# First feed-forward layer in emission order on TensorE, VectorE and ScalarE

## The chip, the cores and the metric

The kernel runs as one program on one NeuronCore of one Trainium2 chip. The metric is the device time of that program in microseconds, start to end on the chip. A short word on the engines, as the profile names them: PE is TensorE (the matrix engine; PEld is its weight load), DVE is VectorE, ACT is ScalarE, POOL is GpSimd, SP is SyncE, which here issues the DMA loads. Each engine works through its own instruction stream in the order in which the stream was written, and waits on semaphores where an instruction needs something from another engine or from a DMA.

## The reference

A two-layer encoder on 256 tokens of 2048 features, all in float32. The layer that the change touches is the channel mixer of layer 0:

```python
def conv_ffn(h, w_up, conv_w, conv_b, w_down):
    gate, up = jnp.split(h @ w_up, 2, axis=-1)
    gp = jnp.pad(gate, ((0, 0), (1, 1), (0, 0)))
    gate = gp[:, :-2] * conv_w[0] + gp[:, 1:-1] * conv_w[1] + gp[:, 2:] * conv_w[2] + conv_b
    return (jax.nn.gelu(gate, approximate=True) * up) @ w_down

for layer in range(DEPTH):                                  # DEPTH = 2
    mod = cond @ ada_w[layer] + ada_b[layer]                # 2048 x 12288, one row
    sh1, sc1, g1, sh2, sc2, g2 = split(mod, 6)
    h = rms_norm(x, norm_g[layer, 0]) * (1.0 + sc1) + sh1
    y = local_dilated_mixer(...) if layer == 0 else diff_attention(...)
    x = x + g1 * rms_norm(y, norm_g[layer, 1])
    h = rms_norm(x, norm_g[layer, 2]) * (1.0 + sc2) + sh2
    y = conv_ffn(h, ...)                                    # hidden width 5504
    x = x + g2 * rms_norm(y, norm_g[layer, 3])
```

## The kernel before

**Weights.** Every weight is read once from HBM. The matrices are cut into *units* of 128 x 1024 float32 (512 KB). A unit is loaded by SP into one of nine `raw` buffers (`load`, L232), split by ACT into a high part `whi` (L259, a rounding copy) and by DVE into the rest `wlo` = `raw` - `whi` (L309), and then used by PE in three matmuls for each product: high times high, high times low, low times high. There are four `whi` and four `wlo` buffers (`SPLIT_BUFS`), so a unit's split can only begin when PE has finished the unit four places earlier; a `raw` buffer is free when its `wlo` is made.

**Modulation.** The rows `mod` are one-row products. They are made from *modulation units*, 128 x 1024 of `ada_w`, also 512 KB and also loaded into the nine `raw` buffers (L236); DVE multiplies each by a column of the condition and adds it to `aacc` (L284; the first of sixteen is L296, or L305 after a start on POOL in L299). Two ticks after the sixteenth, PE sums the partitions (L459 for columns, L451 for gate rows) and DVE takes the result (L471, L474, L453).

**Order.** `Plan.order` writes one list `seq` in which weight units ("w") and modulation units ("a") alternate; in the layer of the change there are 128 "a" to 215 "w", and the last 20 units of the layer have none among them. Loads go out in this order, at most nine ahead (`prefetch`). The program is written as a stream of units: after PE's matmuls of a unit comes `done`, which frees the split buffer, calls `advance` (use up the next entries of `seq`: the copy to `whi` for one "w", the addition to `aacc` for each "a" up to the next "w"), then `tick` (run what is due of the work put off by `chain` and `at`), then `lows` (the `wlo` whose `whi` was just written):

```python
        def done(self, i):
            self.free(i)
            self.advance(lows=False)
            self.tick()
            self.lows()
```

`ada` itself also calls `lows` right after its addition, so where a "w" is followed by an "a", the order written is `whi`, `aacc`, `wlo`, and then the work of the tick.

**The layer.** `ffn(0, ...)` works in two parts of 22 and 21 feature tiles. For each pair of tiles it makes a gate product and an up product (four units each, `feat_units`, matmuls L655, L657, L658 with 256 columns), and then the down product of the part (`out_chunks` with `tok_units`, L622 to L624 with 512 columns, four chunks of 512). The gate product is read from PSUM by ACT (L1051), gets its two outer taps from DVE (L1040, L1042, one tick later), and its gelu from ACT (L1046, two ticks later). The up product is multiplied with it on DVE (L1058), copied to the high part by ACT (L1059) and split by DVE (L1060), a tick apart. The first 7 products (`PRE = 7`) of the layer are made in another loop, in three steps over the contraction; from the eighth on a product is made over its full contraction (L1082 to L1097). Each chunk of the down product is taken by ACT (L1105) in the first part, and by DVE with a sum of squares on ACT (L1108, L491) in the second. The last chunk of the second part ends in `tail`, which makes the norms and the first products of the next layer.

**What sets the order on the engines.** The program is traced into a list of instructions; a list scheduler then decides each engine's order. It runs its own model of the time that each instruction takes, and gives an engine, whenever it is free, the earliest-written instruction that is ready in the model. Within `tc.manual_schedule(engines=ORDERED)`, PE, DVE and ACT instead get the order in which the instructions were written; SP and POOL stay with the list scheduler. In this kernel that is done in one place only, around `tail` (L911).

Of the kernel before, what the change touches and what calls it, by code (L numbers as in the profile page):

```python
# [3 lines left out]

# [5 lines left out]
F32 = mybir.dt.float32  # L10
F32R = mybir.dt.float32r
I32 = mybir.dt.int32
AF = mybir.ActivationFunctionType
# [3 lines left out]
D, S, P = 2048, 256, 128  # L17
KT = D // P
# [19 lines left out]


class Plan:  # L40
    """The order in which weight units and modulation units reach the chip."""

    def __init__(self, ab_w_in, ab_w_out, c_w_in, c_w_out, ffn_w_up, ffn_w_down):
        self.units = []
# [41 lines left out]
                               .rearrange("(a p) n -> p a n", p=P), b, n))  # L86

    def token_chunks(self, w, ks, late=0, lc=2, last=False):
        """512 columns at a time; of the first lc chunks, the last units come after all others"""
        pairs = [ks[i:i + 2] for i in range(0, len(ks), 2)]  # L90
        head = pairs[:len(pairs) - late]
        order = [(ch, head) for ch in range(lc)] + [(ch, pairs[len(head):]) for ch in range(lc)]
        order += [(ch, pairs) for ch in range(lc, 4)]
        for ch, ps in order:
            n = len(self.units)
            for p in ps:
                self.rows(w, p[0], len(p), ch * 512, 512)
            if last and ch == 3:
                u = len(self.units) - n
                skew = min(u, SPLIT_BUFS + HELD)  # L100
                self.held |= set(range(n + u - skew, n + u - SPLIT_BUFS))
# [47 lines left out]
        assert self.ia == len(self.ada)  # L149

    def put(self, nw, na, p=1.0):
        """nw weight units with na modulation units spread among them"""
        e = self.ia + na
        for k in range(nw):
            t = e - na + round(na * ((k + 1) / nw) ** p)
            while self.ia < t:
                self.seq.append(("a", self.ia))
                self.ia += 1
            self.seq.append(("w", self.iw))
            self.iw += 1  # L160
        while self.ia < e:
            self.seq.append(("a", self.ia))
            self.ia += 1
# [25 lines left out]
def encoder_kernel(ctx: ExitStack, tc: tile.TileContext, x, c, ada_w, ada_b, norm_g,  # L189
                   ab_w_in, ab_w_out, a_sink, c_w_in, c_w_out, c_lambda, c_subln_g,  # L190
                   ffn_w_up, ffn_conv_w, ffn_conv_b, ffn_w_down, out):
    nc = tc.nc
# [12 lines left out]
    def vy():  # L205
        return cp.tile([P, 2, D], F32, name="vy")
# [4 lines left out]
    class Stream:  # L211
# [98 lines left out]
            self.los = []  # L310

        def advance(self, limit=None, lows=True, n=None):
            """use up what has been loaded, as far as the split buffers reach"""
            if n is not None:
                limit = self.used + n
            while self.used < len(seq) and (limit is None or self.used < limit):
                kind, i = seq[self.used]
                if kind == "w":
                    if i in plan.held:
                        if self.held_tile is None:  # L320
                            break
                    elif i in plan.native:
                        if self.direct == DIRECT:
                            break
                    elif self.outstanding == SPLIT_BUFS:
                        break
                if kind == "a" and i in plan.gated:
                    if not self.gate:
                        break
                    self.gate -= 1  # L330
                s = self.used
                self.used += 1
                if kind == "w":
                    self.split(s, i)
                else:
                    self.ada(s, i)
                self.prefetch()
            if lows:
                self.lows()
# [9 lines left out]
            return i, self.hl.pop(i)  # L349

        def open(self, n):
            """let n of the gated modulation units through"""
            self.gate += n
            self.advance()

# [15 lines left out]
            self.later.append((self.now + ticks, age, fn))  # L371

        def chain(self, *stages, delay=0):
            """stages one tick after another, each given what the one before returned; older chains go first"""
            age = self.age = self.age + 1

            def run(k, v):
                r = stages[k](v)
                if k + 1 < len(stages):
                    self.at(1, lambda: run(k + 1, r), age)  # L380
            self.at(1 + delay, lambda: run(0, None), age)
# [12 lines left out]
    st = Stream()  # L394
    mods, cur = {}, {}

# [1 line left out]
    def rows_tile():  # L398
        return tmp.tile([P, P], F32, name="crow", bufs=2)

# [33 lines left out]
    nc.vector.memset(mhalf, -0.5)  # L434
    nc.scalar.activation(crow[:KT, :], crow[:KT, :], AF.Silu)

# [1 line left out]
    def gate_rows(l, m):  # L438
        mods[l, m] = cp.tile([P, D], F32, name="gb")
        i0 = 1 if m == 2 else 3  # L440
# [32 lines left out]
                g0 = (l * 4 + (0 if m == 1 else 2)) * KT + k0  # L473
                nc.vector.scalar_tensor_tensor(col, col, 1.0, ngc[:, g0:g0 + n], op0=ALU.add, op1=ALU.mult)  # L474

# [1 line left out]
    def sums():  # L477
        s = small("ssq", 5)
        nc.gpsimd.memset(s[:, 4:5], EPS)
# [16 lines left out]
        return d  # L496

    class Affine:
        """the modulated rows of feature tiles k.. from src, split into high and low parts"""

        def __init__(self, t, k, src, A, B, act, keep=False):
            n = src.shape[1]
# [29 lines left out]
        return dst  # L532

    def chunk_T(t, ch, r, dst):
        """rows 4 ch.. of the normalised and transposed x"""
        z = normed(t, ch, r, tmp.tile([P, 512], F32, name="hf", bufs=3), True)
        nc.scalar.activation(dst, transposed(z, bank()), AF.Copy)

# [1 line left out]
        cur["hT"] = cp.tile([P, KT, 2, S], F32R, name="hT")  # L540

    class Norm:
        """x += gate * rms_norm(y), then the modulated rms_norm of x, transposed and split, for one token block"""

        def __init__(self, t, y, ssq, A=None, B=None):
            self.t, self.y, self.ssq, self.A, self.B = t, y, ssq, A, B
# [65 lines left out]
                for a in self.half:  # L612
                    a.low()

# [1 line left out]
    def mm_tok(dst, act, kt, t, hi, lo, first, last):  # L616
        if lo is None:
            nc.tensor.matmul(dst, cur["h"][:, kt, t * P:(t + 1) * P], hi, start=first, stop=last,
# [5 lines left out]
        nc.tensor.matmul(dst, al, hi, start=False, stop=last, skip_group_check=True)  # L624

    def tok_units(dsts, act, ks, first=True, last=True, one_bank=False):
        """dsts[t] += act block t times the next weights, rows ks"""
        n = 0
        while n < len(ks):
            i, (hi, lo) = st.take()  # L630
            a = hi.shape[1]
            for b in range(a):
                for t in range(2):
                    mm_tok(dsts[t], act, ks[n + b], t, hi[:, b], lo and lo[:, b],
                           first and n + b == 0 and not (one_bank and t), last and n + b == len(ks) - 1)
            n += a
            st.done(i)

    def feat_units(acc, k0, kn, n):
        """one bank: acc[:, j] += (next weights).T @ h for n // 128 feature tiles"""  # L640
        hT = cur["hT"]
        kt = k0
        while kt < k0 + kn:
# [19 lines left out]
    def packed():  # L663
        return bank().rearrange("p (j n) -> p j n", j=2)

# [1 line left out]
    def feat_out(pool, acc, scale, name, bufs=1):  # L667
        q = pool.tile([P, 2, S], F32, name=name, bufs=bufs)
        nc.scalar.activation(q, acc, AF.Copy, scale=scale)
# [13 lines left out]
                                                        op0=ALU.mult, op1=ALU.subtract)  # L683

    def probs_T(pool, parts):
        """the transposed probabilities: parts[t] lists what is summed, each with its normalising diagonal"""
        pt = bank().rearrange("p (k q) -> p k q", k=2)
        for t in range(2):
            for kt in range(2):
# [170 lines left out]

        st.chain(scores, soft, expo, norm, turn, apply, rstd, scaled, back, finish)

# [1 line left out]
    def out_chunks(act, ks, evac, late=0, lc=2, norms=None, late_mods=False, head=None):  # L864
        pairs = [ks[i:i + 2] for i in range(0, len(ks), 2)]
        n = len(ks) - sum(len(p) for p in pairs[len(pairs) - late:]) if late else len(ks)
# [164 lines left out]
    def ffn(l, pool, next_norm, pre=0, head=None, first=()):  # L1031
# [30 lines left out]
        for part, (f0, fn) in enumerate(PARTS):  # L1062
# [3 lines left out]
            for n, (k0, k1) in enumerate(zip(FK, FK[1:])) if p else ():  # L1066
# [7 lines left out]
                for a in range(p):  # L1074
                    feat_units(accs[a], k0, k1 - k0, 2 * P)
                    if k1 == KT:
# [2 lines left out]
                            gate(accs[a], cv, a, 2)  # L1079
                        else:  # L1080
                            up(accs[a], cv, act, a - 1, 2)
            for j in range(p // 2 * 2, fn, 2):  # L1082
                nj = min(2, fn - j)
                for k in range(2):
                    if j + k < p:
                        continue
                    if first:
                        acc = first.pop()
                        feat_units(acc, 4, KT - 4, nj * P)
                    else:  # L1090
                        acc = packed()
                        feat_units(acc, 0, KT, nj * P)
                    if k == 0:
                        cv = pool.tile([P, 2, S], F32, name="cv", bufs=2)
                        gate(acc, cv, f0 + j, nj)
                    else:
                        up(acc, cv, act, j, nj)  # L1097
            final = part == len(PARTS) - 1
            y = y or vy()

            def evac(acc, t, ch, then=None):
                c0 = ch * 512
                yc = y[:, t, c0:c0 + 512]
                if part == 0:
                    nc.scalar.activation(yc, acc, AF.Copy)  # L1105
                    return
                z = tmp.tile([P, 512], F32, name="hf", bufs=3) if final else yc
                nc.vector.tensor_add(z, acc, yc)  # L1108
                if final:
                    square_sum(z, ssq[t][:, ch:ch + 1])  # L1110
                    nc.vector.tensor_mul(yc, z, mods[l, 5][:, c0:c0 + 512])
                if then:
                    then()

            out_chunks(act, list(range(fn)), evac, 0, 0,
                       (lambda: [next_norm(t, y, ssq[t]) for t in range(2)]) if final else None, head=head)

# [1 line left out]
    v_acc, v_got = [], []  # L1119

    def v_units(t, i, k0, hi, lo):
# [197 lines left out]
```

## Time and profile before

| | |
|---|---|
| median of 3 runs | 2326.51 us (2325.22 to 2333.98) |
| profiled execution: span, first to last instruction | 2334.3 us |
| profiled execution: time around the span | not shown on the page |
| PE busy | 2226.5 us (95%) |
| DVE busy | 1620.0 us (69%) |
| ACT busy | 1055.0 us (45%) |
| DMA moved | 587.14 MB, mean 252 GB/s |
| mean granted TensorE clock | 0.980 |

The profile is of one execution. Busy shares are over the whole span, which has stages with different limits. "Idle before" of a group is how long its engine stood still just before instructions of the group, with what ended the wait. In a table of stretches each row gives the stretch's length, each engine's busy time with its number of instructions, the granted TensorE clock (1.00 is full speed), the share of the time that the 16 DMA engines were busy, and the rate. The busy time of PE counts matmuls that overlap, so PE can look busy while it runs below its pace; the number of matmuls in a stretch tells more.

The layer's part that is changed runs from about 460 us to 1160 us of the span: the 7 early products end at about 460 us, the last chunk of the second part and `tail` lie around 1075 to 1160 us.

### The profile page before, as it was taken

To read this page: it belongs to the slowest core of one execution; us is meant where nothing else is said; L and a number is where in the kernel's file an instruction comes from. 1 tells how busy PE (TensorE), PEld (TensorE's weight loads), DVE (VectorE), ACT (ScalarE), POOL (GpSimd) and SP (SyncE) were. 2 spreads that over 40 slices of the span, in tenths; PEclk is the share of its full clock that TensorE was granted. 3 is DMA by queue.
4 is the path that set the end of the run, shared out by engine and by line. 5 is a ranking of instruction groups with operands and counts; after the bars stand their busy time and mean duration, and the time that the engine had idled before them with its cause. 6 is when DMAs were issued, how large, how long until landed. Compare 5 with 4: busy or idle time off the path is not lost.

```text
span 2334.3 us, 37324 instructions
## 1 busy us (share of the span) xinstructions
PE 2226.5 (95%) x14961; PEld 2030.9 (87%) x14961; DVE 1620.0 (69%) x1802; ACT 1055.0 (45%) x1451; POOL 45.5 (2%) x72
## 2 busy tenths in 40 slices
PE   5689999999999999999999999999999999999998
PEld 3679978999877999987888999888999988999986
DVE  7888987887666677776687886657565545565555
ACT  4334455544333334434554554446444444444443
POOL 0000000000000000000000110000000000000000
PEclk8889999999999999999999999999999999999999
DMA  9999989898778888887589996665677666666652
GB/s 343 367 329 318 327 292 316 294 306 287 249 263 273 277 268 270 273 261 265 177 287 334 308 307 212 212 198 162 200 205 203 199 206 207 193 205 201 178 187 104
DMA packets 390427, 587.14 MB, mean 252 GB/s; under 512 B 18110, under 2 KB 256360, under 8 KB 389612
## 3 DMA queue, kind: packets, MB, share of 16 engines
q1 hardware_dynamic: 390252, 584.75, 77.3%
q8 instruction: 117, 1.92, 0.3%
q14 instruction: 58, 0.48, 0.1%
HBM read 582.58 MB, written 2.10 MB: 250 GB/s over the span
## 4 chain that ended last, share of the span: by engine, by line
PE 58%; DMA 17%; issue 13%; DVE 10%; ACT 1%; POOL 1%; DVEq 0%; POOLq 0%; ACTq 0%
DMA raw<-in_ada_w_dram 14%; PE bank L657 11%; PE bank L655 11%; PE bank L658 11%; PE bank L623 7%; PE bank L622 7%; PE bank L624 7%; DVE wlo L309 4%; DVE aacc L284 4%; DMA raw<-in_ffn_w_down_dram 2%; DMA raw<-in_ffn_w_up_dram 1%; PE bank L459 1%; DMA raw<-in_ab_w_in_dram 1%; PE bank L794 1%; PE bank L523 1%
## 5 line engine op out<-in xcount | busy, mean ns | idle before, releaser
L259 ACT ACTIVATE whi<-raw 128x1024 fp32r<-128x1024 f32 x708 | 740.5, 1053 | 873.9 <-PE bank L657 399.6
L309 DVE TENSOR_TENSOR wlo<-raw,whi 128x1024 fp32r<-128x1024 f32 x708 | 856.9, 1217 | 369.3 <-ACT whi L259 356.6
L658 PE MATMUL bank<-hT,wlo 128*128 128x256 f32 x3616 | 1022.7, 283 | 20.1 <-DVE wlo L309 20.0
L655 PE MATMUL bank<-hT,whi 128*128 128x256 f32 x3616 | 1027.9, 284 | 0.0
L657 PE MATMUL bank<-hT,whi 128*128 128x256 f32 x3616 | 1018.8, 282 | 0.2 <-DVE hT L518 0.2
L658 PEld LDWEIGHTS bank<-hT,wlo 128*128 128x128 f32 x3616 | 685.9, 190 | 26.8 <-DVE wlo L309 26.1
L655 PEld LDWEIGHTS bank<-hT,whi 128*128 128x128 f32 x3616 | 686.4, 190 | 3.1 <-ACT whi L259 1.0
L657 PEld LDWEIGHTS bank<-hT,whi 128*128 128x128 f32 x3616 | 686.1, 190 | 3.2 <-issue 1.7
L284 DVE SCALAR_TENSOR_TENSOR aacc<-raw,ccol,aacc 128x1024 f32<-128x1024 f32 x352 | 454.1, 1290 | 209.3 <-DMA raw<-in_ada_w_dram 207.0
L623 PE MATMUL bank<-wlo,act 128*128 128x512 f32 x656 | 261.5, 399 | 12.7 <-DVE wlo L309 12.7
L622 PE MATMUL bank<-whi,act 128*128 128x512 f32 x656 | 259.8, 396 | 0.0
L624 PE MATMUL bank<-whi,act 128*128 128x512 f32 x656 | 259.6, 396 | 0.0
L623 PEld LDWEIGHTS bank<-wlo,act 128*128 128x128 f32 x656 | 123.8, 189 | 48.6 <-DVE wlo L309 20.4
L622 PEld LDWEIGHTS bank<-whi,act 128*128 128x128 f32 x656 | 123.9, 189 | 29.0
L624 PEld LDWEIGHTS bank<-whi,act 128*128 128x128 f32 x656 | 123.9, 189 | 28.5
L622 PE MATMUL bank<-whi,hT 128*128 128x512 f32 (+1 forms) x192 | 76.0, 400 | 14.6 <-ACT hT L514 14.6
L1046 ACT ACTIVATE cv<-cv 128x512 f32<-128x512 f32 (+1 forms) x44 | 27.4, 622 | 106.0 <-DVE cv L1042 105.8
L623 PE MATMUL bank<-wlo,hT 128*128 128x512 f32 (+1 forms) x192 | 75.1, 393 | 0.0
L624 PE MATMUL bank<-whi,hT 128*128 128x512 f32 (+1 forms) x192 | 72.2, 385 | 0.0
L622 PE MATMUL bank<-whi,oT 128*128 128x512 f32 x176 | 71.0, 403 | 0.0
L623 PE MATMUL bank<-wlo,oT 128*128 128x512 f32 x176 | 69.6, 396 | 0.0
L624 PE MATMUL bank<-whi,oT 128*128 128x512 f32 x176 | 69.4, 395 | 0.0
(168 smaller groups left out, 1381.5 us busy)
## 6 DMA issues: line engine op xcount, KB each, us to landing
raw<-in_ada_w_dram SPq DMA_DIRECT2D x384, 512.0 KB, 5.3
raw<-in_ffn_w_up_dram SPq DMA_DIRECT2D x344, 512.0 KB, 4.7
raw<-in_ffn_w_down_dram SPq DMA_DIRECT2D x168, 512.0 KB, 5.2
raw<-in_c_w_in_dram SPq DMA_DIRECT2D x96, 512.0 KB, 5.3
raw<-in_ab_w_in_dram SPq DMA_DIRECT2D x56, 512.0 KB, 6.2
raw<-in_c_w_out_dram SPq DMA_DIRECT2D x32, 512.0 KB, 5.0
raw<-in_ab_w_out_dram SPq DMA_DIRECT2D x16, 512.0 KB, 5.6
gb<-in_norm_g_dram SPq DMA_DIRECT2D x3, 1024.0 KB, 4.8
```

The source lines that it names most:

```text
L259: nc.scalar.activation(hi, v, AF.Copy)
L284: nc.vector.scalar_tensor_tensor(self.acc, t, col, self.acc, op0=ALU.mult, op1=ALU.add)
L309: nc.vector.tensor_tensor(lo, v, hi.bitcast(F32), op=ALU.subtract)
L459: nc.tensor.matmul(t[:, j:j + 1], acc[:, j * P:(j + 1) * P], ones[:, 0:1], start=True, stop=rows is None)
L523: nc.tensor.transpose(ps[:, q * P:(q + 1) * P], src[:, q * P:(q + 1) * P], ident)
L622: nc.tensor.matmul(dst, ah, hi, start=first, stop=False, skip_group_check=True)
L623: nc.tensor.matmul(dst, ah, lo, start=False, stop=False, skip_group_check=True)
L624: nc.tensor.matmul(dst, al, hi, start=False, stop=last, skip_group_check=True)
L655: nc.tensor.matmul(acc[:, j], wh, hT[:, k, 0], start=k == 0 and j == 0, stop=False, skip_group_check=True)
L657: nc.tensor.matmul(acc[:, j], wh, hT[:, k, 1], start=False, stop=False, skip_group_check=True)
L658: nc.tensor.matmul(acc[:, j], wl, hT[:, k, 0], start=False, stop=k == KT - 1, skip_group_check=True)
L1046: nc.scalar.activation(cv[:, :nj], cv[:, :nj], AF.Gelu_apprx_tanh)
```

## The change

The loop over the full-contraction products and the down product, in both parts of layer 0's feed-forward layer, go under `tc.manual_schedule(engines=ORDERED)`. Layer 1 (`pre` is 0 there) and everything else stay as they were. `tail`, which had that context before, now stands within it a second time. Some comments and docstrings are dropped, and an import is added; nothing else differs.

```diff
-from contextlib import ExitStack
+from contextlib import ExitStack, nullcontext
...
-            for j in range(p // 2 * 2, fn, 2):
-                nj = min(2, fn - j)
-                for k in range(2):
...
+            with tc.manual_schedule(engines=ORDERED) if pre else nullcontext():
+                for j in range(p // 2 * 2, fn, 2):
+                    nj = min(2, fn - j)
+                    for k in range(2):
+                        if j + k < p:
+                            continue
+                        if first:
+                            acc = first.pop()
+                            feat_units(acc, 4, KT - 4, nj * P)
+                        else:
+                            acc = packed()
+                            feat_units(acc, 0, KT, nj * P)
+                        if k == 0:
+                            cv = pool.tile([P, 2, S], F32, name="cv", bufs=2)
+                            gate(acc, cv, f0 + j, nj)
+                        else:
+                            up(acc, cv, act, j, nj)
+                final = part == len(PARTS) - 1
+                y = y or vy()
...
+                out_chunks(act, list(range(fn)), evac, 0, 0,
+                           (lambda: [next_norm(t, y, ssq[t]) for t in range(2)]) if final else None, head=head)
```

More of the change, by code (lines that the diff above doesn't have):

```diff
@@ L1081, in ffn @@
                             up(accs[a], cv, act, a - 1, 2)
-            for j in range(p // 2 * 2, fn, 2):
-                nj = min(2, fn - j)
-                for k in range(2):
[L1085 to L1113, printed above, removed]
@@ L1115, in ffn, with evac @@
-            out_chunks(act, list(range(fn)), evac, 0, 0,
-                       (lambda: [next_norm(t, y, ssq[t]) for t in range(2)]) if final else None, head=head)
+            with tc.manual_schedule(engines=ORDERED) if pre else nullcontext():
[17 more added lines that the diff above has]
+                y = y or vy()
+                def evac(acc, t, ch, then=None):
+                    c0 = ch * 512
+                    yc = y[:, t, c0:c0 + 512]
+                    if part == 0:
+                        nc.scalar.activation(yc, acc, AF.Copy)
+                        return
+                    z = tmp.tile([P, 512], F32, name="hf", bufs=3) if final else yc
+                    nc.vector.tensor_add(z, acc, yc)
+                    if final:
+                        square_sum(z, ssq[t][:, ch:ch + 1])
+                        nc.vector.tensor_mul(yc, z, mods[l, 5][:, c0:c0 + 512])
+                    if then:
+                        then()
+                out_chunks(act, list(range(fn)), evac, 0, 0,
+                           (lambda: [next_norm(t, y, ssq[t]) for t in range(2)]) if final else None, head=head)
```

## Prediction

> **What bounds the kernel now.** I read the chain of work that ended last, then the table of stretches, then, for the stretch of the change, the groups, the waits and the order in time on SP and DVE.
>
> ```profile
> span 2334.3 us, 37324 instructions
> PE 58%; DMA 17%; issue 13%; DVE 10%; ACT 1%; POOL 1%; DVEq 0%; POOLq 0%; ACTq 0%
> ```
>
> ```profile
> by line: DMA raw<-in_ada_w_dram 62.6%; DVE wlo L309 14.2%; DVE aacc L284 9.4%; issue 9.4%; DMA raw<-in_ffn_w_up_dram 4.8%; DMA raw<-in_ffn_w_down_dram 3.8%; DVE cv L1058 1.3%; DVE cv L1040 1.0%; DVE aacc L296 0.8%; DVE act L1060 0.6%; DVEq
> ```
>
> The first is the whole span, the second the chain from 560 to 660 us, inside the changed layer: there not PE but the modulation loads and what DVE does after them set the pace. How much PE loses by it comes from the table of stretches and the groups of 512 to 1075 us (the layer from where its waits begin to where PE runs full again).
>
> ```profile
> core 0: us, PE busy (x) PEld busy (x) DVE busy (x) ACT busy (x) POOL busy (x), PEclk, DMA share, GB/s
> 437.00:510.00 73.00, 73.00 (x610) 73.00 (x610) 64.65 (x76) 39.22 (x49) 0.00 (x0) 1.00 0.94 313
> 512.00:1075.00 563.00, 536.60 (x3744) 493.26 (x3744) 389.86 (x397) 222.02 (x253) 0.00 (x0) 0.99 0.84 269
> 1080.00:1130.00 50.00, 50.00 (x217) 40.54 (x216) 33.68 (x33) 24.92 (x30) 0.00 (x0) 1.00 0.78 264
> 1700.00:1800.00 100.00, 100.00 (x855) 100.00 (x854) 59.43 (x67) 46.93 (x53) 0.00 (x0) 1.00 0.69 201
> ```
>
> ```profile
> L658 PE MATMUL bank<-hT,wlo 128*128 128x256 f32 x997 | 283.5, 284 | 13.7 <-DVE wlo L309 13.5
> L623 PE MATMUL bank<-wlo,act 128*128 128x512 f32 x228 | 92.6, 406 | 12.7 <-DVE wlo L309 12.7
> L459 PE MATMUL bank<-ones,aacc 128*128 128x1 f32 x64 | 7.4, 245 | 0.0
> L451 PE MATMUL bank<-aacc,ones 128*128 128x512 f32 x8 | 3.8, 592 | 0.0
> ...
> 513.54 1.72 PE bank L451 x4
> 1240.57 1.68 PE bank L459 x16
> ```
>
> The last two are pieces of the chain. The 3744 matmuls of the stretch are three times 997 and 228, within three, and 72 small ones. Undisturbed, a 256-column matmul takes 100 / 855 = 0.1170 us (1700 to 1800, the same product in layer 1) or 73 / 610 = 0.1197 (437 to 510, this layer, modulation units beside it); a 512-column one 50 / 217 = 0.2304. So PE needs 2989 x 0.1170 = 349.7 to 2989 x 0.1197 = 357.8, plus 683 x 0.2304 = 157.4, plus four L459 groups at 1.68 and two L451 groups at 1.72, 10.2: 517.3 to 525.4 us of the 563. It loses 38 to 46 us, 42 in the middle. What PE waits for is `wlo`; the waits of the stretch say why that is late.
>
> ```profile
> DVE aacc L284 <- DMA raw<-in_ada_w_dram: 157.8, 83, 4.3
> ACT cv L1046 <- DVE cv L1042: 95.5, 15, 8.2
> ACT act L1059 <- DVE cv L1058: 70.7, 17, 6.3
> PE bank L658 <- DVE wlo L309: 13.5, 18, 2.8
> PE bank L623 <- DVE wlo L309: 12.7, 16, 1.8
> ```
>
> DVE stands before `aacc` until a modulation load lands; behind it wait `wlo`, the taps and the product of the up half; ACT stands before gelu and the copy to `act`, and behind these wait the next `whi`. And why is the load late, with nine buffers? SP's queue:
>
> ```profile
> 495.65 0.34 SPq L236 DMA_DIRECT2D raw<-in_ada_w_dram  x1
> 496.85 0.37 SPq L232 DMA_DIRECT2D raw<-in_ffn_w_up_dram  x1
> 498.58 0.34 SPq L236 DMA_DIRECT2D raw<-in_ada_w_dram  x1
> 499.78 2.05 SPq L232 DMA_DIRECT2D raw<-in_ffn_w_up_dram  x2
> 504.34 0.34 SPq L236 DMA_DIRECT2D raw<-in_ada_w_dram  x1
> ...
> 570.45 0.34 SPq L236 DMA_DIRECT2D raw<-in_ada_w_dram  x1
> 574.36 1.50 SPq L232 DMA_DIRECT2D raw<-in_ffn_w_up_dram  x2
> ```
>
> and DVE's order:
>
> ```profile
> 504.62 1.28 DVE L284 SCALAR_TENSOR_TENSOR aacc<-raw,ccol,aacc 128x1024 f32<-128x1024 f32 x1
> ...
> 575.70 1.28 DVE L284 SCALAR_TENSOR_TENSOR aacc<-raw,ccol,aacc 128x1024 f32<-128x1024 f32 x1 [0.24 <-DMA raw<-in_ada_w_dram]
> ```
>
> I paired loads and additions in order of time. The load of 495.65 is used at 504.62, 9.0 us and five issues later, with no wait; the load of 570.45 at 575.70, 5.2 us and two issues later, as soon as it lands. `seq` would put eight issues between. The scheduler has moved the additions forward past `wlo` that were not yet ready in its model, until each meets its own load in flight; the slot that it frees goes to the next load, which is then as late.
>
> **The change, part by part.** It adds and removes no work, on any engine or queue; it puts PE, DVE and ACT in written order from about 460 to 1160 us. Both parts and the token products share one answer, so I cost them together.
>
> *DVE.* `aacc` goes back to its place in `seq`: up to eight other loads are issued between a load and its use. The costs beside this:
>
> ```profile
> L309 DVE TENSOR_TENSOR wlo<-raw,whi 128x1024 fp32r<-128x1024 f32 x181 | 216.8, 1214 | 6.3 <-ACT whi L259 6.3
> L284 DVE SCALAR_TENSOR_TENSOR aacc<-raw,ccol,aacc 128x1024 f32<-128x1024 f32 x103 | 132.2, 1283 | 158.2 <-DMA raw<-in_ada_w_dram 157.8
> L1042 DVE SCALAR_TENSOR_TENSOR cv<-bank,cwc,cv 128x255 f32<-128x255 f32 x31 | 14.9, 481 | 0.7
> L1040 DVE SCALAR_TENSOR_TENSOR cv<-bank,cwc,cv 128x255 f32<-128x255 f32 x31 | 14.7, 476 | 0.0
> L259 ACT ACTIVATE whi<-raw 128x1024 fp32r<-128x1024 f32 x181 | 186.2, 1052 | 165.1 <-PE bank L624 85.6 <-PE bank L657 67.6 <-DVE wlo L309 5.2
> ```
>
> The middle PE need, 521 us for 181 units, is 2.88 us a unit; the nine slots then hold 5.6 units with their additions, 16 us. A load takes:
>
> ```profile
> raw<-in_ffn_w_up_dram SPq DMA_DIRECT2D x115, 512.0 KB, 5.1
> raw<-in_ada_w_dram SPq DMA_DIRECT2D x108, 512.0 KB, 4.6
> ...
> raw<-in_ffn_w_up_dram SPq DMA_DIRECT2D x26, 512.0 KB, 5.3
> raw<-in_ada_w_dram SPq DMA_DIRECT2D x15, 512.0 KB, 5.9
> ```
>
> (512 to 1075 us, then 437 to 510): 5 to 6 us of the 16, so the 157.8 us of waits should go, and with them the 95.5 and 70.7 on ACT. The new waits: `wlo` stands behind `whi`, which stands behind PE's end of the unit four back, and now no addition can slip in between. Cover: from that end to the unit's use are three units, 3 x 2.88 = 8.6 us; `whi` and `wlo` take 1.05 + 1.21 = 2.3, so 6.3 are spare. The worst ordinary burst ahead of a `wlo`, an addition and four taps, takes 1.28 + 4 x 0.48 = 3.2. In all, DVE's 389.86 us are 75% of 521, ACT's 222.02 43%: both have room. Cost zero; were the cover gone, it is the slow rival below.
>
> *PE.* The L459 and L451 groups keep their place two ticks after the last addition; a unit behind them waits if DVE is behind. Nothing shows PE waiting for an addition in this stretch; bounded by 0 and, for the six groups, one addition of 1.28 us each, 7.7 us. I take 1, since DVE has room.
>
> *SP and POOL* stay with the scheduler. SP's loads follow the slots that DVE frees: additions give theirs back later than now, so the weights are loaded less far ahead, but still the 16 us above. The rate must rise: 563 x 269 = 151.4 MB in 521 us are 291 GB/s. The 437 to 510 row, with 26 weight loads to 15 modulation loads, moved 313 with PE never idle; at 0.94 share to 0.84, so there is room. Cost zero, bounded by the whole 42 (a rival). POOL has nothing in the stretch.
>
> *After the layer*, the scheduler's model starts from other times, and its choices in the rest may differ. No row prices that; the longest single waits of PE above are 1.8 and 2.8 us, and one or two of these more or less make the plus or minus 4 that I put into the range.
>
> *The clock.* Of the 42, part is PE's clock:
>
> ```profile
> 604.00:608.00 4.00, 1.20 (x10) 0.99 (x9) 2.97 (x4) 0.00 (x0) 0.00 (x0) 0.99 0.31 79
> 608.00:611.40 3.40, 3.40 (x18) 3.40 (x18) 3.40 (x6) 1.06 (x2) 0.00 (x0) 0.50 0.85 283
> ```
>
> After a wait of about 2.8 us came 3.4 us at half clock, 1.7 us lost; I expect this to go with the wait. [...]
>
> *Sum.* 42 - 1 - 2 (an allowance for the first units in the new order, about one PE wait) = 39 us. Against the profiled execution: 2334.3 - 39 = 2295 us of span, and what lies around it is not shown. That span is 7.8 over the median of the runs, 2326.5; I take the same 39 off that: **2287 us**, with 2277 to 2300 for this case (46 gained and 4 better after; 38 gained, less 7.7 for the PE groups and 4 for the later stages).
>
> **The rivals.** *Half remains* (2306 us): the layer keeps half of its PE waits, 21 us, because gelu and the copy to `act` still stand on ACT ahead of `whi`. For: such waits are 166 us now. Against: they end on DVE instructions that end on a DMA; from 437 to 510, with the early lead, PE stood still for nothing.
>
> *No change* (2326): the loads are late because the DMA engines give no more than 269 GB/s beside this work, and not because of DVE's order. For: a share of 0.84 and 5 us landings. Against: 313 above, with the same mix.
>
> *Slower* (2341): DVE's written order. A gate's four taps, an addition and the two steps of the up half before it meet one `wlo` and exceed the spare 6.3 us, at each of the layer's 16 gates of the stretch (31 tap pairs). It decides from 42 / 16 = 2.6 us of PE wait per gate; at 3.5, 56 are lost for 42 gained. Against: the burst above is 3.2. [...]
>
> **How the numbers follow.** As forecast 0.66; half 0.15; no change 0.10; slower 0.09. About 0.5%, 12 us, is what a measurement of this kernel can tell from none: faster means below 2315, slower above 2338. The first two are faster, 0.81; same 0.10; slower 0.09. The range 2277 to 2315 holds the first two.
>
> **What would show it.** Waits of `aacc` for its loads near zero and five or more issues between load and use; gelu and the `act` copy waiting well under their 95.5 and 70.7; 512 to about 1034 us with the same 3744 matmuls; 285 GB/s or more; PE at 1.00. Wrong: `aacc` still behind its load (no change), DVE waiting for `whi` while PE waits for `wlo` (slower), or the time from the layer's end on differing by over 4 us.

## The result and the profile after

The changed kernel takes 2290.33 us (median of 2286.19 to 2296.29) against 2327.65 for the kernel before (2325.22 to 2333.98): ratio 0.9845, 95% interval 0.9821 to 0.9869. Forecast were 2287 us and 2277 to 2315. The medians differ by 37.3 us. The profiled execution has a span of 2294.5 us, forecast 2295.

The page of the changed kernel, its span and its chain by engine:

```profile
span 2294.5 us, 37387 instructions
PE 80%; issue 12%; DVE 4%; DMA 3%; ACT 1%; POOL 1%; DVEq 0%; POOLq 0%; ACTq 0%
```

DMA goes from 17% of the chain to 3, DVE from 10 to 4. The chain of the changed kernel between 560 and 660 us, which before was modulation loads to 63%:

```profile
by line: PE bank L658 23.1%; PE bank L657 23.1%; PE bank L655 23.1%; PE bank L622 9.8%; PE bank L623 9.8%; PE bank L624 9.5%; PE bank L451 1.7%
```

Now it is matmuls only. The table of stretches of the changed kernel, with the same columns as before (length, busy time and instructions of PE, PEld, DVE, ACT, POOL, granted clock, DMA share, GB/s):

```profile
512.00:1036.00 524.00, 524.00 (x3747) 491.88 (x3746) 398.57 (x401) 229.81 (x258) 0.00 (x0) 1.00 0.88 291
...
1036.00:2294.00 1258.00, 1236.83 (x8146) 1127.74 (x8144) 797.43 (x900) 588.54 (x810) 29.49 (x38) 0.99 0.67 215
```

and the last stretch of the kernel before:

```profile
1075.00:2334.00 1259.00, 1237.50 (x8150) 1127.98 (x8148) 799.44 (x904) 591.67 (x815) 29.62 (x38) 0.99 0.68 215
```

The 3744 matmuls that took 563 us now take 524 (3747 of them), at a granted clock of 1.00; the rest of the kernel takes the same time as before. PE's order is the same in both traces, so matmuls can be compared one by one: the one that starts at 512 us in the changed kernel starts within 0.3 us of that in the kernel before, the one at 1036 us 40.0 us later. So the whole gain, 39 to 40 us of these executions, comes from the layer. The waits in this stretch of the changed kernel (engine, line, what it waited for, us in all, times, longest):

```profile
ACT whi L259 <- PE bank L657: 164.3, 101, 3.6
DVE wlo L309 <- ACT whi L259: 115.0, 152, 2.5
ACT whi L259 <- PE bank L624: 90.9, 53, 3.5
...
DVE mod L471 <- PE bank L459: 8.3, 4, 2.3
ACT cv L1046 <- DVE cv L1042: 3.2, 9, 0.4
```

No wait of `aacc` for a load is left (157.8 us before), gelu waits 3.2 us (95.5 before), and the copy to `act` and PE's matmuls are not in the list any more. What ACT waits for now is PE, and DVE waits for ACT. In SP's queue and in DVE's order of the changed kernel, one load and its use:

```profile
564.50 0.34 SPq L236 DMA_DIRECT2D raw<-in_ada_w_dram  x1
566.19 3.25 SPq L232 DMA_DIRECT2D raw<-in_ffn_w_up_dram  x2
570.26 0.34 SPq L236 DMA_DIRECT2D raw<-in_ada_w_dram  x1
571.99 0.37 SPq L232 DMA_DIRECT2D raw<-in_ffn_w_up_dram  x1
573.79 0.34 SPq L236 DMA_DIRECT2D raw<-in_ada_w_dram  x1
574.93 3.32 SPq L232 DMA_DIRECT2D raw<-in_ffn_w_up_dram  x2
```

```profile
577.77 1.28 DVE L284 SCALAR_TENSOR_TENSOR aacc<-raw,ccol,aacc 128x1024 f32<-128x1024 f32 x1
```

Load at 564.50, use at 577.77: 13.3 us and six other issues later (the second of the last two was issued after the addition began), and no wait in front of it. Paired in order of time, the loads between 560 and 660 us have a median of 13.0 us and a mean of 6.2 issues to their use; before, 5.1 us and 1.9. The 5.1 us hold the wait in front of the addition; without it 3.4 us are left in the median (520 to 1030 us). Counted in the traces, 90 of 98 additions between 520 and 1030 us stood five `wlo` ahead of their written place in the kernel before; the shift grew from 0 to 3 between 460 and 520 us, then to five, and stayed there.

### The profile page after: what moved, and what is told of

It is laid out like the page before. It is cut to its first block, busy times and chain, and to the rows that moved or that the text cites. A ratio compares the mean times of both kernels' runs of the same rounds, so it can differ in the third digit from the quotient of the medians.

```text
span 2294.5 us, 37387 instructions
## 1 busy us (share of the span) xinstructions
PE 2214.2 (97%) x14961; PEld 2030.4 (88%) x14961; DVE 1626.6 (71%) x1802; ACT 1059.6 (46%) x1451; POOL 45.3 (2%) x72
## 4 chain that ended last, share of the span: by engine, by line
PE 80%; issue 12%; DVE 4%; DMA 3%; ACT 1%; POOL 1%; DVEq 0%; POOLq 0%; ACTq 0%
PE bank L655 16%; PE bank L657 16%; PE bank L658 16%; PE bank L622 9%; PE bank L624 9%; PE bank L623 9%; DVE aacc L284 2%; DMA raw<-in_ada_w_dram 2%; PE bank L459 1%; DVE wlo L309 1%; DMA raw<-in_ab_w_in_dram 1%; PE bank L523 1%; PE bank L831 1%; PE bank L794 0%; ACT junk L491 0%
## 5 line engine op out<-in xcount | busy, mean ns | idle before, releaser
L309 DVE TENSOR_TENSOR wlo<-raw,whi 128x1024 fp32r<-128x1024 f32 x708 | 861.2, 1219 | 488.6 <-ACT whi L259 472.6
L658 PE MATMUL bank<-hT,wlo 128*128 128x256 f32 x3616 | 1018.8, 282 | 5.4 <-DVE wlo L309 5.4
L658 PEld LDWEIGHTS bank<-hT,wlo 128*128 128x128 f32 x3616 | 685.2, 189 | 7.1 <-DVE wlo L309 7.0
L284 DVE SCALAR_TENSOR_TENSOR aacc<-raw,ccol,aacc 128x1024 f32<-128x1024 f32 x352 | 453.8, 1289 | 49.3 <-DMA raw<-in_ada_w_dram 47.5
L623 PE MATMUL bank<-wlo,act 128*128 128x512 f32 x656 | 258.9, 395 | 0.0
L623 PEld LDWEIGHTS bank<-wlo,act 128*128 128x128 f32 x656 | 123.5, 188 | 28.5
L623 PE MATMUL bank<-wlo,hT 128*128 128x512 f32 (+1 forms) x192 | 75.2, 394 | 0.0
L623 PE MATMUL bank<-wlo,oT 128*128 128x512 f32 x176 | 69.6, 395 | 0.0
L486 POOL TENSOR_TENSOR rs_r<-rs_m,mhalf 128x1 f32<-128x1 f32 x32 | 25.6, 809 | 1902.6 <-DVE rs_m L484 1902.6
```

Of the source, the lines that this page charges most:

```text
L284: nc.vector.scalar_tensor_tensor(self.acc, t, col, self.acc, op0=ALU.mult, op1=ALU.add)
L309: nc.vector.tensor_tensor(lo, v, hi.bitcast(F32), op=ALU.subtract)
L486: nc.gpsimd.tensor_tensor(r, m, mhalf, op=ALU.pow)
L623: nc.tensor.matmul(dst, ah, lo, start=False, stop=False, skip_group_check=True)
L658: nc.tensor.matmul(acc[:, j], wl, hT[:, k, 0], start=False, stop=k == KT - 1, skip_group_check=True)
```

## The experiments

**Which engine's order it is.** PE's instructions stand in the same order in both kernels, so only DVE's and ACT's can matter. One run orders DVE alone, one the two others.

```diff
-with tc.manual_schedule(engines=ORDERED) if pre else nullcontext():
+with tc.manual_schedule(engines={ENG.DVE}) if pre else nullcontext():                    # dve_only
+with tc.manual_schedule(engines={ENG.PE, ENG.Activation}) if pre else nullcontext():     # pe_act
```

> Layer 0's feed-forward part with DVE alone in written order; PE and ACT go back to the scheduler. Theory (the place of the additions in DVE's order is the cause, and ACT's long waits only followed from it): the whole gain stays, 2290 us (2285 to 2296), no wait of aacc for its loads, about six issues between load and use. Rival (ACT's written order is needed as well, because gelu and the copy to act stand ahead of whi): half the gain goes, 2300 to 2312 us, with PE waiting for wlo again.

> The complement: PE and ACT in written order, DVE left to the scheduler. Theory (DVE's order is the cause): the time of the kernel before, 2327 us (2318 to 2335), two issues between load and use, aacc waiting over 100 us for loads. Rival (ACT's order does part of it): 2300 to 2315 us.

DVE alone: 2289.44 us, 0.9856 of before (0.9839 to 0.9873), the whole gain. PE and ACT alone: 2320.96, 0.9982 (0.9967 to 0.9996); by its interval 1 to 8 us belong to ACT's order. The waits of 512 to 1036 us with PE and ACT ordered and DVE not:

```profile
DVE aacc L284 <- DMA raw<-in_ada_w_dram: 135.7, 80, 4.6
...
ACT cv L1046 <- DVE cv L1042: 70.3, 14, 7.8
PEld bank L623 <- DVE wlo L309: 16.7, 16, 1.8
PEld bank L658 <- DVE wlo L309: 14.1, 19, 1.3
ACT act L1059 <- DVE cv L1058: 12.7, 10, 2.0
```

ACT's order takes most of the wait of the `act` copy away (12.7 of 70.7 left) and it is worth almost nothing, because DVE still stands before its loads. The theory holds, the rival falls.

**Which of DVE's instructions.** Here the list scheduler orders every engine again; only the additions are tied, each behind the `wlo` written before it.

```diff
+    self.last_lo = nc.vector.tensor_tensor(lo, v, hi.bitcast(F32), op=ALU.subtract)      # in lows
...
+    with tc.issue_after(self.last_lo.ins) if self.pin else nullcontext():                # in ada
         nc.vector.scalar_tensor_tensor(self.acc, t, col, self.acc, op0=ALU.mult, op1=ALU.add)
...
-with tc.manual_schedule(engines=ORDERED) if pre else nullcontext():
+with nullcontext():                                                # pin is True in this part only
```

> No written order in this part at all; the scheduler orders all engines, but each addition (L284 of the kernel before) in it is held behind the wlo that was written just before it. Theory (the additions were moved ahead of earlier wlo): nearly the whole gain, 2288 to 2300 us, five or more issues between load and use. Rival (the gain is in the order of all DVE work, taps and products too): under half of it, 2310 to 2327 us.

2288.83 us, 0.9852 (0.9836 to 0.9867). About a hundred ties do what ordering three engines did. The stretch with the additions tied:

```profile
512.00:1036.00 524.00, 524.00 (x3746) 491.99 (x3745) 397.98 (x400) 231.40 (x258) 0.00 (x0) 1.00 0.88 291
```

**How far an addition may move.** The same ties, but to the `wlo` three places earlier.

```diff
-    with tc.issue_after(self.last_lo.ins) if self.pin else nullcontext():
+    with tc.issue_after(self.lo_list[-1 - 3].ins) if self.pin else nullcontext():
```

> As the pin run, but each addition is held behind the wlo three places before the one written just ahead of it, so that it may stand up to three wlo early. In the kernel before, 90 of 98 additions between 520 and 1030 us stand five early, in the changed kernel none. Theory (an addition may move forward as long as its load still has the time to land): three units of 2.88 us off the 12.9 us of the changed kernel leave 4.3, a little under the 5.3 us of landing; waits of about 1 us each, 40 to 110 us in all, mostly inside the cover of wlo, so PE loses 0 to 12 us and the kernel takes 2288 to 2301 us. Rival (each place forward costs alike): three fifths of the 40 us, 2307 to 2320 us.

2289.82 us, 0.9854 (0.9829 to 0.9878): no loss. 99 of 104 additions stand three early. The loads have 7.6 us and three issues, not the 4.3 us that I worked out: a place costs 1.8 us of lead and not a unit's 2.88, presumably because with the additions out of the way the next loads go out sooner, which was not shown. The waits of 512 to 1036 us with additions three early (lines here are one or two higher; L260 is `whi`):

```profile
ACT whi L260 <- DMA raw<-in_ffn_w_up_dram: 57.4, 33, 2.7
ACT whi L260 <- DMA raw<-in_ffn_w_down_dram: 22.6, 14, 1.8
...
DVE aacc L298 <- DMA raw<-in_ada_w_dram: 5.4, 4, 2.3
```

It is now the weights that land just in time, on ACT, with PE waiting for nothing. In the kernel before, with five places, the order leaves the 3.4 us given above, below the 4.6 us in which its loads land, and DVE waited 157.8 / 83 = 1.9 us for each of 83 loads. So the cost sets in somewhere between three and five places; four was not tried, and whether it comes at once or by degrees is not shown.

**Fewer buffers.** The changed kernel with seven, six and five `raw` buffers everywhere.

```diff
-RAW_BUFS, SPLIT_BUFS, HELD = 9, 4, 4
+RAW_BUFS, SPLIT_BUFS, HELD = 7, 4, 4          # 6 and 5 in the other two
```

> The changed kernel with seven raw buffers in place of nine, everywhere. Theory (what counts is that a load has more issues ahead of its use than its 5 to 6 us of landing): four issues and 8 to 9 us between load and use in layer 0's feed-forward part, where PE then loses under 8 us; other stages are not foreseen. Rival (the lead of nine buffers is only just enough): aacc waits over 40 us for its loads there and PE loses over 20 us in that part.

> The changed kernel with six raw buffers. Theory: three issues, about 6.3 us between load and use, just over the 4.6 to 5.4 us of landing that seven buffers showed: aacc waits under 15 us in layer 0's feed-forward part and PE loses under 6 us there. Rival (the loads' scatter needs more): 15 to 40 us of PE lost there.

> The changed kernel with five raw buffers in place of nine, everywhere. Theory (it is the issues between a load and its use that count, not the written order as such): two issues and 4 to 4.5 us are left, as short as the scheduler's order left with nine buffers; aacc waits 40 to 150 us for its loads in layer 0's feed-forward part, PE loses 20 to 60 us there, and the kernel takes over 2330 us. Rival (the written order helps in itself): PE loses under 10 us there.

One time each: 2301.30, 2309.78 and 2353.07 us. But the layer loses nothing in any of them. With five buffers, the stretch and the wait for loads:

```profile
512.00:1036.00 524.00, 524.00 (x3905) 498.62 (x3905) 402.27 (x405) 232.39 (x260) 0.00 (x0) 1.00 0.89 293
```

```profile
DVE aacc L284 <- DMA raw<-in_ada_w_dram: 11.2, 18, 1.9
```

(more matmuls than above because the stretch lies earlier in this layer). With five, the theory was wrong about the layer: the rival said under 10 us lost, and none were. The time of over 2330 us that the theory gave came true all the same, for a reason that it did not name. Issues between load and use are 4.1, 3.1 and 2.3, the times 8.9, 7.6 and 5.6 us. So the count of issues, which I had used as the measure, is not it: 1.9 issues and 2.3 issues lie side by side, one with 157.8 us of waits and one with 11.2. What tells the two apart is the time that the order leaves without the wait itself: 3.4 us against a landing of 4.6 in the kernel before, 5.6 us against 5.1 with five buffers. That the kernel slows all the same comes from elsewhere: the first copy to `act` of the changed kernel and of the one with five buffers (start of the first and the last, behind the durations):

```profile
L1059 ACT ACTIVATE act<-cv x44: 398/616/637, 450.3 to 2169.0; 128x512 fp32r<-128x512 f32 x42, 128x256 fp32r<-128x256 f32 x2
```

```profile
L1059 ACT ACTIVATE act<-cv x44: 400/617/634, 489.8 to 2225.8; 128x512 fp32r<-128x512 f32 x42, 128x256 fp32r<-128x256 f32 x2
```

39.5 us are lost ahead of this point, and 17 more (1736.0 against 1718.7 us) behind it. Compared matmul by matmul with the changed kernel, five buffers are 40.9 us late where that kernel is at 512 us, 39.7 at 1036, 39.6 at 1130 and 58.3 at 1450: nothing is lost in the layer, and the rest goes in layer 1's attention.

**How much cover DVE has.** The changed kernel with one `wlo` per gate product made several times over, to lengthen the burst ahead of it.

```diff
-                nc.vector.tensor_tensor(lo, v, hi.bitcast(F32), op=ALU.subtract)
+                for _ in range(1 + self.extra):                     # taps() sets extra: 6, or 3
+                    nc.vector.tensor_tensor(lo, v, hi.bitcast(F32), op=ALU.subtract)
+                self.extra = 0
```

> The changed kernel with one wlo per gate product of layer 0's main loop made seven times over (six more of 1.21 us, 7.3 us of DVE, some 17 times), to see how much cover the written order has on DVE. Theory: the cover is 6.3 us at a time, and DVE's busy share of 0.78 in the up and gate products goes over 1.0, so PE waits for wlo by 20 to 45 us in all, 2310 to 2335 us. Rival (the cover is larger than thought, since weights are split ahead): under 10 us lost.

> The changed kernel with one wlo after each of the 18 gate products under the written order made four times over (three more of 1.21 us, 3.6 us of DVE each, 65 us in all). Theory (a cover of 6.3 us for each unit, DVE's busy share in the up and gate products from 0.78 to 0.94): PE loses under 6 us in that part, 2286 to 2298 us. Rival (the cover is smaller, or a burst is not made up before the next): over 1 us per gate, 2308 us or more.

Six more took 2384.43 us, far above the 2310 to 2335 that the theory gave, and three more 2300.14, above the theory's 2286 to 2298 and below the rival's 2308. Six more also reached the four gates of the early products, 22 gates in all (852 `wlo` in place of 720); three more reached one of them, 19 in all (777 `wlo`). What I had left out of both sums is the ordinary burst of 3.2 us that stands there already: 7.3 + 3.2 - 6.3 = 4.2 us a gate, times 22 is 92 us, and 94 were lost; 3.6 + 3.2 - 6.3 = 0.5 us, times 19 is 10 us, and 10 were lost. But I made these sums after the runs, each on one time, and the traces divide the loss in another way, so the agreement is luck. PE's waits between 437 and 1130 us with six more, then with three more:

```profile
PE bank L661 <- DVE wlo L311: 47.2, 18, 8.1
PE bank L454 <- DVE aacc L285: 7.1, 2, 5.7
PE bank L462 <- DVE aacc L285: 5.7, 1, 5.7
PE bank L626 <- DVE wlo L311: 4.0, 2, 2.6
```

```profile
PE bank L454 <- DVE aacc L285: 1.8, 1, 1.8
PE bank L462 <- DVE aacc L285: 1.8, 1, 1.8
PE bank L661 <- DVE wlo L311: 1.1, 1, 1.1
```

(L661, L626, L454, L462, L311 and L285 are L658, L623, L451, L459, L309 and L284 moved.) With six more, PE waits 51.2 us for `wlo` and 12.8 us for additions in front of a sum over the partitions, and between 458 and 1100 us its granted clock is at half for 65 us in all, which costs up to 32. With three more it waits for a `wlo` once, 1.1 us; most of its loss stands at two sums that wait for an addition and at 6.8 us of half clock behind one of them. So the runs do not measure the cover as 6.3 us. They show that a burst longer by 3.6 us is covered at 18 of 19 gates, and that one longer by 7.3 us is not. The slow rival's mechanism is real, and the kernel's own bursts stay under its point.

**The next stage.** Layer 1's attention has 64 modulation loads too. One run puts it in written order on the three engines, on top of the change; the two others tie the additions, there (and in the layer), or in the whole kernel, with no order written out.

```diff
     with tc.tile_pool(name="at1", bufs=1, reuse_waits="tile") as pool:
+        with tc.manual_schedule(engines=ORDERED):                   # at1_all; the body one level in
...
-            st.pin = False                                          # pin_at1: the tie goes on to ffn(1)
```

> The changed kernel, and layer 1's attention with its projections in written order on PE, DVE and ACT too (64 modulation loads beside about 66 weight loads there). Theory (the same early additions cost there too; 3 to 5 us pieces of modulation loads stand in the chain between 1308 and 1451 us): 8 to 20 us less than the changed kernel, 2270 to 2282 us. Rival (the steps of the attention heads, each a short chain over four engines, wait for each other in written order): slower than the changed kernel by 5 to 30 us, 2295 to 2320 us.

> As the pin run (the scheduler orders everything, each L284 addition held behind the wlo written before it, in layer 0's feed-forward part), and the same hold in layer 1's attention too. Theory (there too the additions run ahead and meet their loads in flight, 34.5 us of such waits between 1130 and 1570 us, while the heads' steps may still fill in): 3 to 12 us less than the pin run, 2277 to 2286 us. Rival (those waits lie beside PE's waits for the heads' own chain, or the hold makes additions block the softmax steps as the full written order did): 2286 to 2310 us.

> The same hold for every L284 addition of the kernel, layer 0's attention included. Theory: layer 0's attention has under 15 us of such waits, so the time of the run that holds them from the feed-forward part on, within 5 us. Rival (in the first 140 us the additions are the work and PE waits for them, so a hold behind a wlo delays the start): 10 us or more slower than that run.

In written order: 2315.96 us, 0.9962 (0.9948 to 0.9976), 26 us slower than the changed kernel. With the additions tied: 2283.73, 0.9816 (0.9802 to 0.9831), the fastest of all kernels here, and 5 us below the run with the tie in the layer alone (its interval 0.9836 to 0.9867 lies above). Tied everywhere: 2286.04, 0.9824 (0.9807 to 0.9841), no further gain. One hundred microseconds inside the attention, first with the tie in the layer alone, then in the attention too:

```profile
1350.00:1450.00 100.00, 95.59 (x710) 90.48 (x709) 68.79 (x91) 48.25 (x90) 5.09 (x7) 1.00 0.68 220
```

```profile
1350.00:1450.00 100.00, 100.00 (x731) 94.46 (x731) 77.27 (x102) 52.55 (x98) 5.13 (x7) 1.00 0.73 236
```

The hundred before these, in the changed kernel, then with the attention in written order; and in the latter the longest wait of PE between 1130 and 1570 us:

```profile
1250.00:1350.00 100.00, 98.44 (x774) 95.44 (x773) 90.62 (x112) 52.49 (x97) 11.13 (x10) 1.00 0.91 301
```

```profile
1250.00:1350.00 100.00, 91.53 (x682) 86.64 (x681) 75.92 (x92) 45.35 (x82) 13.16 (x10) 0.97 0.79 256
```

```profile
PE bank L822 <- DVE smc L815: 14.0, 10, 3.3
```

The tie gets 731 matmuls into its stretch in place of 710 and takes 33.5 us of waits of `aacc` for loads away. The written order cures these waits as well, but gets 682 in place of 774 into its own; PE waits 14.0 us for the softmax of a head (5.3 in the changed kernel): where an order written step by step holds the short steps of a head one behind another, the list scheduler's freedom seems worth more than it cost. That the 14.0 us and what followed are the whole of the 26 was not shown.

## Why the prediction was right

**PE's need.** Worked out: 517 to 525 us for the stretch, 521 in the middle. Measured: 524 with no wait of PE. The need itself is thus 3 us above the middle. The two allowances, 1 us for the PE groups and 2 us for the first units, were for waits that did not come, so that they add up to the same 3 us, and the 39 us to the point, is luck.

**DVE's order is the cause.** Held: ordering DVE alone gives the whole gain, tying the additions alone too. ACT's long waits followed from it, as said: with DVE alone ordered, gelu waits 5.6 us (95.5 before) and the copy to `act` 3.1 (70.7). With this the rival in which half of the waits remain on ACT falls.

**The lead.** Right in direction, off in size: the step that put eight issues and 16 us between load and use is the mis-sized one. It measured 6.1 issues and 12.9 us (520 to 1030 us). The loads do not go out when they are written but when the `wlo` or the addition in their slot is done: SP's queue waits 283.0 us for `wlo` and 86.8 us for additions between 512 and 1036 us. The reasoning by issues in that step also fell in the runs with fewer buffers; the time left for the landing stands in its place.

**The cover of `wlo`.** It is enough, as worked out: between 512 and 1036 us of the changed kernel PE waits for no `wlo`, and a burst longer by 3.6 us is still covered at 18 of 19 gates. The figure of 6.3 us itself is not shown.

**The rate.** 291 GB/s forecast, 291 measured, at a share of 0.88. The no-change rival, that 269 GB/s were the limit, falls.

**The clock.** The granted clock is 1.00 in the whole stretch, and PE has no wait there: the half clock went with the waits, as the prediction expected. In the kernel before it was 0.50 for 3.4 us twice, from 608.0 us behind a PE gap of 2.80 us and from 1044.9 us behind one of 1.79 us; the prediction had seen the first.

**After the layer.** Put at plus or minus 4 us; 1258 against 1259 us measured.

**PE in written order.** Nothing, since its order did not change; priced at 1. The wait that this price was for comes where DVE is made later: with three more `wlo` at a gate, PE waits 1.8 us for an addition in two places.

## What to carry to other kernels

Where a list scheduler fills an engine's idle time with work that is ready in its model, look at what that work waits for on the chip. In the kernel before, an addition moved forward onto its load in flight started at 573.04 us, after 2.62 us of waiting for it; the `wlo` behind it ran at 574.25, though its `whi` was done by 569.79. Such waits for loads were 157.8 us on DVE between 512 and 1075 us, and with DVE alone reordered gelu's wait on ACT fell from 95.5 to 5.6 us. Compare the time from a load's issue to its use, less the wait in front of the use, with the landing time: 3.4 against 4.6 us in the kernel before. Where it is shorter, one tie that keeps the early instruction behind its neighbour can be worth as much as writing out the order of three engines (2288.83 us here against 2290.33), and it leaves the scheduler free where its filling helps (2283.73 us against 2315.96 in the attention). A ring of buffers does not give a long lead by its size: with the same nine buffers the time from load to use was 5.1 us in one order and 13.0 in the other.

## What the runs showed of the hardware that I had not expected

Half-megabyte loads land in about 5 us whether two or six others are issued between load and use: the medians of the modulation loads are 4.6 us in the kernel before, 5.3 in the changed one, 4.6 with seven buffers and 5.1 with five, at 269 to 293 GB/s. And with five buffers in place of nine the written order still runs PE at full pace at 293 GB/s: four buffers fewer cost this stage nothing, though the stages before and after it lose 57 us.

Half clock also came behind PE gaps shorter than the 2.80 us that the prediction had seen: 1.79 us at 1042.3 us of the kernel before was followed by 3.4 us at 0.50, and 1.81 us at 825.1 us of the run with three more `wlo` by 6.8 us of half clock. Not every gap under 2 us was followed by it: after 1.94 us at 1445.7 us of the changed kernel the clock stayed at 1.00.
